# Hybrid trunk on one core: joined repairs, negated scores, one order of the attention on TensorE

## The chip, the cores and the metric

One core of a Trainium2 chip runs the kernel. Its engines are TensorE (PE in the profile; its weight loads are PEld), VectorE (DVE), ScalarE (ACT), GpSimd (POOL) and SyncE (SP), which issues the DMA transfers here. The metric is the device time of one launch in microseconds, as the median of several runs.

## The reference

The kernel computes two layers of a trunk over 256 latent tokens `x` and 256 context tokens `h`, with a width of 1024. In each layer every part is normalized and modulated, `_rms_norm(x, g) * (1 + scale) + shift`, where shift, scale and gate are nine vectors that come from `silu(c) @ ada_w[l] + ada_b[l]`:

```python
x = x + 0.5 * m[2] * swiglu(modulate(x, norm_g[l, 0], m[0], m[1]), w1, w3, w2)      # width 2816
o = concat(hgrn2(...), neighbourhood_attention(...), sliding_window_attention(...)) # of modulate(x) @ w_in
x = x + m[5] * (o @ w_out[l])
x = x + 0.5 * m[8] * swiglu(modulate(x, norm_g[l, 2], m[6], m[7]), ...)
```

The context goes the same way, and in the last layer only as far as the latents need it. Neighbourhood attention (NA) has six heads of 64: a latent query sees all four rows of its grid, within a row the columns of a window of 16, and all context keys; its scores are `q·k/8 + bias`, with a bias `na_rpb` by relative position and a mask of −1e30 elsewhere. Sliding-window attention (SW) has six query heads on two key heads, rotary positions, a window of 128 to each side and one sink score for each head that enters the softmax's maximum and sum. All inputs are float32.

## The kernel before, in words

The program is written out by hand, line by line, and a scheduler orders it when the kernel is built: it goes by the program's order, by dependences and by priorities. Pools (28 slots, 12 half tiles, four PSUM tiles `mm` for products, four `aux`) decide when a tile is free again. What the program pins (`keep_in_program_order`) keeps its place on its engine.

**Products.** Each float32 product is three matmuls on rounded parts (`mm3`, L222 to L226): whi·h, wlo·h and whi·(rest of h), 128x512 each over eight steps k. `Stream` (L68) reads weights in transfers of up to 1 MB into three buffers; `convert` (L100) makes a unit's `whi` on ScalarE (L109) and `wlo` on VectorE (L110), some five units ahead.

**Startup** (`body`, L1071; `boot`, L1153; `first`, L418). x and context are transposed on TensorE, eight groups of four into `xps` (L1140), and copied by VectorE into `xT` (L1142). Then VectorE's short chain gives `rs` (L397 to L402), which `rbc` spreads over partitions (L1274). `ada_direct` (L308) makes one block of 512 modulation columns: eight matmuls `adaps` with the transferred `adaraw` (L314), a ScalarE copy `adaev`, four small matmuls `adap` (L320) and VectorE's additions. Blocks 2 and 0 are scale and shift of the first four steps k, blocks 3 and 1 those of the last four. `first` multiplies four units at once: for k = 0 it calls `boot(0)`, for k = 4 `boot(1)`.

**FFN** (`ffn`, L475). Pairs of product groups for w1 and w3; ScalarE's silu (L522), VectorE's product `silu` (L523), the split `g` (L219, L220), then w2. Beside it runs `side`: `ada_gen` (L323) accumulates further modulation columns on VectorE (`adaacc`, L347 and L349) with matmuls at the end of each, and `load_bias(l)` (L1039) reads layer l's bias: one transfer into `scr`, 24 transfers `bias<-scr` on the SP queue (L1051), and one POOL instruction of 128x3072 that adds the column mask `colmask` (L1054). `tick` takes steps of these jobs by credits.

**Mixer** (`mixer`, L1015). `proj_hg` first; then `weave` mixes three threads by their costs: projections (`proj_v_na` L627, `proj_sw` L686, `w_out` L970), `hgrn` (L723), and `attention` (L873) for "na", then "sw", with an earlier priority. Attention goes over units (j, qt): head pairs j = 0 to 2, query tiles qt of 128, 0 and 1 latent, 2 and 3 context (mixer 1 has only the first two). `stage_s` makes a head's scores (two matmuls, `ks` and `kls`, L891 and L892) and the softmax: VectorE adds bias or mask and takes the maximum (L903, into a half tile `sb`; for context L908), makes it negative (L910; with the sink L913), ScalarE's exponential with the sum (L914), the reciprocal (L918) and the scale (L919). `stage_t` transposes P (`pt`, L927) and copies it to `ptsb`, on ScalarE for the first head of a pair (L930), on VectorE for the second (L932). `stage_v` multiplies by V into `ot` (L946), and the last unit of a pair is split into `o`. In a step, for each head the scores of unit i and the transposes of unit i − 1 follow each other, then stage_v of unit i − 2. Some lines of it:

```python
            for hh in range(2):
                if i < n:
                    stage_s(i, hh)
                    yield 0.5
                if 0 <= i - 1 < n:
                    stage_t(i - 1, hh)
                    yield 0.5
            if 0 <= i - 2 < n:
                stage_v(i - 2)
                yield 0.9
```

## Time and profile before

| | |
|---|---|
| time, median of 3 runs | 1890.07 us (1888.53 to 2241.34) |
| the profiled execution's own time | 1889.66 us |
| its span | 1887.9 us |
| TensorE busy | 1839.9 us, 97% |
| VectorE, ScalarE, POOL busy | 67%, 38%, 7% |
| chain that ended last | PE 89%, DVE 4%, ACT 2%, DMA 2% |

The profile is of one execution. A row of the timeline has the start in us from the span's start, its duration, the engine, the line of the kernel, the operation with its output and inputs, how often it is repeated and, in brackets, the engine's idle time before it and what ended that. Times of successive matmuls overlap in these rows, so the distance of starts tells their pace. The clock is the share of full speed that TensorE was granted.

### The profile page before, as it was taken

The page shows a single profiled execution, that of the slowest core. Times are in us where ns is not written, and L with a number is a line of the kernel's source. Part 1 is how long each engine was busy: PE and PEld are TensorE (multiplying, and loading weights), DVE is VectorE, ACT ScalarE, POOL GpSimd, SP SyncE. Part 2 cuts the span into 40 slices and gives each one's busy share as a digit, 9 for nine tenths or more (in the row PEclk, how much of TensorE's full clock was granted, in tenths as well). Part 3 has the DMA queues.
Part 4 walks back from the last instruction along what each step waited for, and adds up shares of the span by engine and source line. Part 5 has one row for each costly group of instructions (what it writes and reads, how often), then busy time and mean ns, then how long its engine had stood idle before and what let it go on. Part 6 is the DMA issues. An engine that isn't in the chain of part 4 may idle for free.

```text
span 1887.9 us, 27747 instructions
## 1 busy us (share of the span) xinstructions
PE 1839.9 (97%) x11071; PEld 1521.7 (81%) x11071; DVE 1266.0 (67%) x2341; ACT 725.2 (38%) x1214; POOL 138.5 (7%) x199
## 2 busy tenths in 40 slices
PE   7999999999999899999999999999999999999998
PEld 4777778789777679778777897777888977789998
DVE  4696668766777778867567675565333757887554
ACT  4322222235346457322222362222123635665443
POOL 0100000030400102000000110000001140020000
PEclk9999999999999999999999999999999999999999
DMA  9664545532211123645445426564222321146651
GB/s 346 197 218 148 184 156 178 168 116 69 74 49 40 34 71 102 214 154 192 142 146 193 128 86 205 171 203 161 90 95 76 120 68 38 43 154 203 214 168 56
DMA packets 233642, 258.24 MB, mean 137 GB/s; under 512 B 18886, under 2 KB 195370, under 8 KB 233258
## 3 DMA queue, kind: packets, MB, share of 16 engines
q1 hardware_dynamic: 233514, 256.48, 42.4%
q8 instruction: 87, 1.43, 0.3%
q14 instruction: 41, 0.34, 0.1%
HBM read 255.41 MB, written 2.48 MB: 137 GB/s over the span
## 4 chain that ended last, share of the span: by engine, by line
PE 89%; DVE 4%; ACT 2%; DMA 2%; issue 1%; SPq 1%; POOL 1%; DVEq 0%; ACTq 0%; POOLq 0%
PE mm L224 27%; PE mm L225 27%; PE mm L226 26%; PE ot L946 2%; PE pt L927 1%; DMA adaraw<-in_ada_w_dram 1%; PE adaps L359 1%; PE s L891 1%; DVE adaacc L349 1%; PE s L892 1%; PE lv L747 1%; POOL k L774 1%; ACT whi L109 1%; DVE P L919 0%; DMA raw<-in_ffn_w_dram 0%
## 5 line engine op out<-in xcount | busy, mean ns | idle before, releaser
L224 PE MATMUL mm<-h,whi 128*128 128x512 f32 (+1 forms) x1632 | 594.6, 365 | 5.4 <-DVE silu L523 3.2
L225 PE MATMUL mm<-h,wlo 128*128 128x512 f32 (+1 forms) x1632 | 590.4, 362 | 0.0
L226 PE MATMUL mm<-h,whi 128*128 128x512 f32 (+1 forms) x1632 | 589.4, 361 | 0.0
L110 DVE TENSOR_TENSOR wlo<-raw,whi 128x1024 fp32r<-128x1024 f32 (+2 forms) x344 | 400.2, 1184 | 90.5 <-ACT whi L109 75.5
L109 ACT ACTIVATE whi<-raw 128x1024 fp32r<-128x1024 f32 (+2 forms) x344 | 338.8, 1012 | 291.7 <-PE mm L225 131.1
L224 PEld LDWEIGHTS mm<-h,whi 128*128 128x128 f32 x1632 | 307.8, 189 | 68.1 <-issue 12.6
L225 PEld LDWEIGHTS mm<-h,wlo 128*128 128x128 f32 x1632 | 308.1, 189 | 50.3 <-issue 1.5
L226 PEld LDWEIGHTS mm<-h,whi 128*128 128x128 f32 x1632 | 308.0, 189 | 50.2 <-issue 0.2
L349 DVE SCALAR_TENSOR_TENSOR adaacc<-adaraw,s,adaacc 128x512 f32<-128x512 f32 x392 | 281.6, 763 | 40.4 <-DMA adaraw<-in_ada_w_dram 39.1
L224 PE MATMUL mm<-g,whi 128*128 128x512 f32 (+1 forms) x740 | 265.1, 358 | 0.0
L226 PE MATMUL mm<-g,whi 128*128 128x512 f32 (+1 forms) x740 | 263.7, 356 | 0.0
L225 PE MATMUL mm<-g,wlo 128*128 128x512 f32 (+1 forms) x740 | 263.5, 356 | 0.0
L219 ACT ACTIVATE g<-silu 128x512 fp32r<-128x512 f32 (+1 forms) x92 | 51.4, 562 | 317.4 <-DVE silu L523 284.5
L523 DVE TENSOR_TENSOR silu<-mm,silu 128x512 f32<-128x512 f32 (+1 forms) x80 | 50.0, 629 | 165.1 <-PE mm L226 139.0
L415 DVE SCALAR_TENSOR_TENSOR xT<-mm,mod,xT 128x256 f32<-128x256 f32 x216 | 96.7, 479 | 94.1 <-PE mm L226 93.3
L224 PEld LDWEIGHTS mm<-g,whi 128*128 128x128 f32 x740 | 139.1, 188 | 24.9 <-ACT whi L109 2.5
L225 PEld LDWEIGHTS mm<-g,wlo 128*128 128x128 f32 x740 | 139.1, 188 | 21.7
L226 PEld LDWEIGHTS mm<-g,whi 128*128 128x128 f32 x740 | 139.1, 188 | 21.6
L1243 POOL CAST hp<-mod 128x2 fp32r<-128x2 f32 x40 | 22.7, 598 | 1114.3 <-PE mm L225 339.0
L522 ACT ACTIVATE silu<-mm 128x512 f32<-128x512 f32 (+1 forms) x80 | 42.6, 547 | 132.0 <-PE mm L226 132.0
L220 DVE TENSOR_TENSOR g<-silu,g 128x512 fp32r<-128x512 f32 (+1 forms) x92 | 54.8, 603 | 32.1 <-ACT g L219 31.8
L1225 POOL TENSOR_TENSOR ssq<-ssq,sq 128x256 f32<-128x256 f32 x50 | 44.5, 904 | 302.9 <-ACT sq L1222 302.8
(210 smaller groups left out, 2008.3 us busy)
## 6 DMA issues: line engine op xcount, KB each, us to landing
raw<-in_ffn_w_dram SPq DMA_DIRECT2D x120, 1024.0 KB, 5.5
adaraw<-in_ada_w_dram SPq DMA_DIRECT2D x144, 512.0 KB, 5.0
raw<-in_ffn_w_dram SPq DMA_DIRECT2D x16, 768.0 KB, 5.0
raw<-in_w_in_dram SPq DMA_DIRECT2D x12, 1024.0 KB, 5.1
raw<-in_w_in_dram SPq DMA_DIRECT2D x16, 512.0 KB, 5.1
raw<-in_w_out_dram SPq DMA_DIRECT2D x8, 640.0 KB, 3.9
bias<-scr SPq DMA_DIRECT2D x48, 64.0 KB, 2.4
raw<-in_w_in_dram SPq DMA_DIRECT2D x4, 768.0 KB, 4.6
```

Of the source, the lines that this page charges most:

```text
L109: K.nc.scalar.activation(hi, v, AF.Copy)
L110: K.nc.vector.tensor_tensor(out=lo, in0=v, in1=hi.bitcast(F32), op=OP.subtract)
L219: self.nc.scalar.activation(hi, src, AF.Copy)
L220: self.nc.vector.tensor_tensor(out=lo, in0=src, in1=hi.bitcast(F32), op=OP.subtract)
L224: mmul(ps, whi, ahi, start=start, stop=False)
L225: mmul(ps, wlo, ahi, start=False, stop=False)
L226: mmul(ps, whi, alo, start=False, stop=stop)
L349: nc.vector.scalar_tensor_tensor(acc[:, t], w, sc, acc[:, t], op0=OP.mult, op1=OP.add)
L415: self.nc.vector.scalar_tensor_tensor(self.x[:, d, sl], ps[:, sl], self.mod[l][:, m, d, s:s + 1], self.x[:, d, sl], op0=OP.mult, op1=OP.add)
L522: nc.scalar.activation(a[:, 0:n], ps[i][:, 0:n], AF.Silu)
L523: nc.vector.tensor_tensor(out=a[:, 0:n], in0=ps[2 + i][:, 0:n], in1=a[:, 0:n], op=OP.mult)
L1225: eng.tensor_tensor(out=self.ssq[s], in0=self.ssq[s], in1=t, op=OP.add)
```

## The change

Four parts, and an order for each.

1. Startup. `pinned` makes matmuls, transposes and conversions keep program order. Only four groups of x transposes stand ahead of `rs`; two follow block 2, two block 0, the last two with late copies. `ada_direct` loses its second half to `ada_columns`, called later. k 0 to 3 of units 0 and 1 come first, and blocks 3 and 1 are laid among k 0 to 3 of units 2 and 3.
2. Bias. The POOL instruction goes; VectorE makes `bias = colmask − bias` in six pinned pieces of 128x512 in each layer. The `scr` transfer is pinned too. The side jobs are 2 to 4, bias, 5 to 8 instead of 2 and 3, bias, 4 to 8, and the bias costs more credits.
3. Signs. Scores, masks, bias and sink are stored negated (q is scaled by −0.125), so that VectorE takes a minimum and the exponential gets scale −1; the instruction that made the maximum negative goes for "na". P overwrites the masked scores in place of `sb`. `hgrn` uses `K2` for its output instead of a new slot.
4. Attention on TensorE. Scores wait (without a semaphore, `behind`) for the fourth k of the projection after theirs (`R.marks`), transposes for the last scores issued. A step makes both heads' scores, then both heads' transposes; `stage_v` takes two units at a time, heads 1, 0, pinned. Both copies to `ptsb` are ScalarE's.

```diff
-            for k in range(KC):
-                if k == 0:
-                    us = norm.boot(0)
-                elif k == 4:
-                    norm.boot(1)
-                    norm.bounds()
-                for u, p in zip(us, ps):
-                    self.mm3(p, u[0][:, k], u[1][:, k], norm.h[k][:, 0], norm.h[k][:, 1], k == 0, k == KC - 1)
+            for k in range(4):
+                prod(k, 0, 1)
+            scale = norm.block(3)
+            prod(0, 2, 3)
+            self.ada_columns(0, 3, scale)
+            prod(1, 2, 3)
+            prod(2, 2, 3)
+            shift = norm.block(1)
+            prod(3, 2)
+            self.ada_columns(0, 1, shift)
+            prod(3, 3)
+            norm.boot2()
+            norm.bounds()
+            for k in range(4, KC):
+                prod(k, 0, 1, 2, 3)
+                self.st.pump()
...
-                    R.q["na"] += self.stack_q(ps, n, 0.125)
+                    R.q["na"] += self.stack_q(ps, n, -0.125)
...
-            nc.tensor.matmul(ps[:, 0:nk], q[:, qs], k[:, k0:k0 + nk], start=True, stop=False)
-            nc.tensor.matmul(ps[:, 0:nk], q[:, qs], kl[:, k0:k0 + nk], start=False, stop=True)
+            ins = nc.tensor.matmul(ps[:, 0:nk], q[:, qs], k[:, k0:k0 + nk], start=True, stop=False)
+            if qt == 0 and hh == 0:
+                self.behind(ins, R.marks[mark(i)])
+            last.append(nc.tensor.matmul(ps[:, 0:nk], q[:, qs], kl[:, k0:k0 + nk], start=False, stop=True))
...
-                src = self.half("sb")
+                src = P
...
-                                               scalar=-3e38, op0=OP.add, op1=OP.max, accum_out=mx)
+                                               scalar=3e38, op0=OP.add, op1=OP.min, accum_out=nmx)
...
-            if kind == "na":
-                nc.vector.tensor_scalar(nmx, mx, -1.0, None, op0=OP.mult)
-            else:
+            if kind == "sw":
                 sk = self.sink[:, l * 6 + h:l * 6 + h + 1]
-                nc.vector.tensor_scalar(nmx, mx, sk, -1.0, op0=OP.max, op1=OP.mult)
-            nc.scalar.activation(P[:, 0:nk], src[:, 0:nk], AF.Exp, bias=nmx, accum_out=tot)
+                nc.vector.tensor_scalar(nmx, nmx, sk, None, op0=OP.min)
+            nc.scalar.activation(P[:, 0:nk], src[:, 0:nk], AF.Exp, bias=nmx, scale=-1.0, accum_out=tot)
...
-            if hh == 0:
-                nc.scalar.activation(pt[:, 0:nk], ps[:, 0:nk], AF.Copy)
-            else:
-                nc.vector.tensor_copy(pt[:, 0:nk], ps[:, 0:nk])
+            nc.scalar.activation(pt[:, 0:nk], ps[:, 0:nk], AF.Copy)
...
+            for hh in range(2):
                 if 0 <= i - 1 < n:
                     stage_t(i - 1, hh)
                     yield 0.5
-            if 0 <= i - 2 < n:
-                stage_v(i - 2)
-                yield 0.9
+            if i >= 3 and i % 2 == 1:
+                stage_v((i - 2, i - 3))
+                yield 1.8
...
-        nc.gpsimd.tensor_tensor(out=self.bias[:, 0:12, :], in0=self.bias[:, 0:12, :], op=OP.add,
-                                in1=self.colmask[:, None, :].to_broadcast([128, 12, 256]))
+        for h in range(6):
+            b = self.bias[:, 2 * h:2 * h + 2, :]
+            self.tc.keep_in_program_order(
+                nc.vector.tensor_tensor(out=b, in0=self.colmask[:, None, :].to_broadcast([128, 2, 256]), in1=b,
+                                        op=OP.subtract))
+            yield 1
...
-        self.ada_it = self.side((0, [2, 3]), (0, None), (0, [4, 5, 6, 7, 8]))
+        self.ada_it = self.side((0, [2, 3, 4]), (0, None), (0, [5, 6, 7, 8]))
```

TensorE at startup, from `rbc` to the first product matmuls, before (`adaps` are the eight matmuls of a block, in the order 2, 0, 3; `adap` its columns):

```order
L1274 MATMUL rbc<-cc,rs 128x128 x4
L314 MATMUL adaps<-adaraw,s_153 32x512 x8
L320 MATMUL adap_251<-cc,adaev 128x2 x4
L314 MATMUL adaps<-adaraw,s_153 32x512 x8
L320 MATMUL adap_269<-cc,adaev 128x2 x4
L314 MATMUL adaps<-adaraw,s_153 32x512 x8
L224 MATMUL mm<-h,whi 128x512 x2
```

And after the change (all matmuls of the helper stand at L227, `xps` at L1197):

```order
L1354 MATMUL rbc<-cc,rs 128x128 x4
L227 MATMUL adaps<-adaraw,s_153 32x512 x8
L1197 MATMUL xps<-cc,xraw 128x128 x8
L227 MATMUL adaps<-adaraw,s_153 32x512 x8
L227 MATMUL adap_247<-cc,adaev 128x2 x4
L227 MATMUL adap_258<-cc,adaev 128x2 x4
L1197 MATMUL xps<-cc,xraw 128x128 x8
L227 MATMUL mm<-h,whi 128x512
```

The third block, whose matmuls stood right ahead of the first product, has moved behind 24 of them, and half of the x transposes have moved in behind `rbc`.

TensorE in mixer 0, where the first attention units stand, before (`s_` are score tiles, one for each head and unit, `mm_4301` a projection, `pt_` transposes of P):

```order
L892 MATMUL s_4327<-kls_4292,qs_4200 128x512
L224 MATMUL mm_4301<-h_3186,whi_4104 128x512
L225 MATMUL mm_4301<-h_3186,wlo_4105 128x512
L226 MATMUL mm_4301<-h_3186,whi_4104 128x512
L892 MATMUL s_4316<-kls_4292,qs_4200 128x512
L224 MATMUL mm_4301<-h_3187,whi_4104 128x512
L225 MATMUL mm_4301<-h_3187,wlo_4105 128x512
L226 MATMUL mm_4301<-h_3187,whi_4104 128x512
L224 MATMUL mm_4301<-h_3188,whi_4104 128x512
L225 MATMUL mm_4301<-h_3188,wlo_4105 128x512
L226 MATMUL mm_4301<-h_3188,whi_4104 128x512
L927 MATMUL pt_4338<-cc_83,P_4309 128x128 x4
```

And after the change:

```order
L227 MATMUL mm_4283<-h_3170,whi_4086 128x512
L933 MATMUL s_4310<-ks_4273,qs_4182 128x512
L936 MATMUL s_4310<-kls_4274,qs_4182 128x512
L933 MATMUL s_4319<-ks_4273,qs_4182 128x512
L933 MATMUL s_4328<-ks_4273,qs_4182 128x512
L936 MATMUL s_4328<-kls_4274,qs_4182 128x512
L933 MATMUL s_4337<-ks_4273,qs_4182 128x512
L936 MATMUL s_4319<-kls_4274,qs_4182 128x512
L936 MATMUL s_4337<-kls_4274,qs_4182 128x512
L969 MATMUL pt_4346<-cc_83,P_4314 128x128 x4
L969 MATMUL pt_4353<-cc_83,P_4323 128x128 x4
L933 MATMUL s_4360<-ks_4273,qs_4182 128x256
```

The projection matmuls that stood between the scores and the first transposes have moved ahead of the scores; eight score matmuls of two units now stand in a row, and the transposes follow them.

VectorE in the second FFN after the change, where layer 1's mask goes on (`bias<-cc,bias`; `silu` and `g` belong to the FFN's products):

```order
L557 TENSOR_TENSOR silu<-mm,silu 128x512
L222 TENSOR_TENSOR g<-silu,g 128x512
L110 TENSOR_TENSOR wlo<-raw,whi 128x1024
L1110 TENSOR_TENSOR bias<-cc,bias 128x512
L110 TENSOR_TENSOR wlo<-raw,whi 128x1024
L1110 TENSOR_TENSOR bias<-cc,bias 128x512 x4
L110 TENSOR_TENSOR wlo<-raw,whi 128x1024
L1110 TENSOR_TENSOR bias<-cc,bias 128x512
L365 TENSOR_SCALAR adaacc<-adaraw,s_153 128x512 x2
```

Before, POOL did this in mixer 0, behind the last hgrn instructions of that mixer:

```order
L774 TENSOR_TENSOR k_3144<-k_3144,tot 128x16x16 x2
L774 TENSOR_TENSOR k_3145<-k_3145,tot 128x16x16 x2
L774 TENSOR_TENSOR k_3144<-k_3144,tot 128x8x32 x2
L774 TENSOR_TENSOR k_3145<-k_3145,tot 128x8x32 x2
L1054 TENSOR_TENSOR bias<-bias,cc 128x3072
L1243 CAST hp<-mod_141 128x2 x2
```

It has moved from POOL to VectorE and from mixer 0 to the FFN behind it.

## Rows read from the trace of the kernel before

**Rows 1.** The head of the page and its first part.
```profile
span 1887.9 us, 27747 instructions
...
PE 1839.9 (97%) x11071; PEld 1521.7 (81%) x11071; DVE 1266.0 (67%) x2341; ACT 725.2 (38%) x1214; POOL 138.5 (7%) x199
```

**Rows 2.** Waits of TensorE by releaser: total us, times, longest us.
```profile
PE pt L927 <- DVE sm L918: 7.4, 2, 5.4
PE lv L747 <- DVE q L774: 3.7, 3, 2.0
```

**Rows 3.** Timeline, startup: start us, us, engine line op out<-in xcount [idle before <-releaser].
```profile
13.47 2.48 DVE L1142 COPY xT<-xps 128x512 f32<-128x512 f32 x4
...
28.60 1.05 PE L314 MATMUL adaps<-adaraw,s 128*32 128x512 f32 x4 [1.73 <-DMA adaraw<-in_ada_w_dram]
...
30.16 4.62 DVE L110 TENSOR_TENSOR wlo<-raw,whi 128x1024 fp32r<-128x1024 f32 x4
...
33.55 0.74 PE L224 MATMUL mm<-h,whi 128*128 128x512 f32 x2
```

**Rows 4.** Timeline, around k = 4 of the first group.
```profile
49.57 1.05 PE L320 MATMUL adap<-cc,adaev 128*128 128x2 f32 x8 [0.77 <-ACT adaev L317]
...
52.22 0.79 PE L224 MATMUL mm<-h,whi 128*128 128x512 f32 x1 [1.60 <-ACT h L1293]
```

**Rows 5.** Timeline, SP's queue, VectorE and TensorE in the first FFN.
```profile
51.17 14.81 SPq L1051 DMA_DIRECT2D bias<-scr  x17
...
80.78 9.96 DVE L349 SCALAR_TENSOR_TENSOR adaacc<-adaraw,s,adaacc 128x512 f32<-128x512 f32 x5
...
102.98 0.77 PE L224 MATMUL mm<-h,whi 128*128 128x512 f32 x1 [3.23 <-DVE silu L523]
```

**Rows 6.** Timeline, end of mixer 0's attention: repair, scale, transpose.
```profile
631.46 6.99 POOL L1054 TENSOR_TENSOR bias<-bias,cc 128x3072 f32<-128x3072 f32 x1 [122.21 <-DMA bias<-scr]
...
631.95 6.65 DVE L919 TENSOR_SCALAR P<-P,sm 128x256 f32<-128x256 f32 x1
...
638.75 0.66 PE L927 MATMUL pt<-cc,P 128*128 128x128 f32 x2 [5.36 <-DVE sm L918]
```

**Rows 7.** Timeline, one head's softmax chain in mixer 0.
```profile
536.41 0.42 PE L892 MATMUL s<-kls,qs 128*128 128x512 f32 x1
...
536.86 0.69 DVE L903 CUSTOM_DVE_ANT_1 sb<-s,bias 128x512 f32<-128x512 f32 x1 [0.59 <-PE s L892]
...
538.55 1.28 ACT L914 ACT_TABLE_LOAD   x1 [1.05 <-DVE sm L910]
...
539.84 0.72 ACT L914 ACTIVATE P<-sb,sm 128x512 f32<-128x512 f32 x1
...
542.31 0.63 PE L927 MATMUL pt<-cc,P 128*128 128x128 f32 x4 [1.16 <-DVE P L919]
```

**Rows 8.** Windows: A:B length, busy us (x count) by engine, PEclk, DMA share, GB/s.
```profile
105.00:110.00 5.00, 5.00 (x16) 3.94 (x15) 5.00 (x7) 2.88 (x4) 0.00 (x0) 0.61 0.33 120
...
640.00:645.00 5.00, 5.00 (x22) 3.00 (x22) 1.77 (x8) 1.29 (x5) 0.00 (x0) 0.52 0.01 3
```

**Rows 9.** Timeline of TensorE, last neighbourhood attention units in mixer 0.
```profile
623.77 0.70 PE L717 MATMUL rot<-swraw,cc 128*128 128x256 f32 x2 [0.69 <-ACT swraw L701]
...
627.97 0.43 PE L946 MATMUL ot<-ptsb,v 128*64 128x128 f32 x2 [1.46 <-ACT ptsb L930]
628.33 0.51 PE L224 MATMUL mm<-o,whi 128*128 128x512 f32 x1
628.68 0.40 PE L225 MATMUL mm<-o,wlo 128*128 128x512 f32 x1
628.91 0.39 PE L226 MATMUL mm<-o,whi 128*128 128x512 f32 x1
```

**Rows 10.** Lines: copies of transposed tiles; xcount | busy us, mean ns | idle before.
```profile
L932 DVE COPY ptsb<-pt 128x512 f32<-128x512 f32 (+1 forms) x36 | 21.4, 595 | 11.2 <-PE pt L927 11.2
...
L930 ACT ACTIVATE ptsb<-pt 128x512 f32<-128x512 f32 (+1 forms) x36 | 18.5, 515 | 10.4 <-PE pt L927 10.1
```

178 lines of the change are left out of this document (117 added, 61 removed).

## Prediction

> **What bounds the kernel now.** I read the page first: TensorE is busy for 1839.9 of the span's 1887.9 us [rows 1]. So the time is TensorE's own work, the 48 us in which it waits, and the work that it does at the lower granted clock after a wait. The change leaves the number of TensorE instructions as it is (10051 in the order before and after), so it can win only the 48 us, the clock, and the small price of going from one kind of matmul to another. Next I read the waits of TensorE, summed by who ended them: the largest are transposes of P behind a VectorE instruction and hgrn's `lv` behind VectorE and, through it, POOL [rows 2]. Then I went through the timeline at each pause: the startup [rows 3, 4], one pause in the first FFN [rows 5] and the end of mixer 0's attention [rows 6]. Last the windows, for the clock: 105 to 110 us ran at a mean of 0.61 and 640 to 645 us at 0.52, with TensorE busy all the time [rows 8]. The level in between is a mixture of 1.2 and 2.4 GHz; a busy window of 5 us at mean c has lost (1 − c) × 5 us, so 1.95 and 2.4 us here. Each of these two windows follows a pause of TensorE of over 3 us.
>
> The profiled execution took 1889.66 us, 0.4 less than the median of the runs shown; the sum below starts from it.
>
> **Startup.** Before, the x transposes' eight copies stand ahead of the chain that gives `rs`, which the scale of every h needs; the last four take 2.48 us from 13.47 [rows 3]. With four of them moved behind, `rs` comes some 2.4 us earlier, and with it the columns and h; by nothing if the adaraw transfers are what is late. No wait on them stands in the rows before 28.60, so I take the earlier h. The first product matmul stands at 33.55 because all eight matmuls of block 3 stand ahead of it in program order and wait for adaraw from 28.60 on [rows 3]. Afterwards 24 product matmuls (k 0 to 3 of two units) stand ahead of block 3. They need h, and whi and wlo of two units; wlo x4 ran from 30.16 for 4.62 us [rows 3], so I let them begin at 29. Up to k = 4 TensorE then has 48 product matmuls of 0.23 us (11.1 us; spacing in [rows 9]), blocks 3 and 1 of twice 1.05 us [rows 3] (4.2), two sets of columns of 1.05 [rows 4] (2.1), with 3 to 6 matmuls laid over each adaev copy, and I add 1.2 for the clock, half of what the worse window lost [rows 8]: 18.6 us. So k = 4 starts at about 47.6, where it was 52.22 after pauses of 0.77 and 1.60 us [rows 4]: −4.6. After 52.22 the clock was lower for a while too; of a loss like that of [rows 8] I count 1.4, since a pause remains. **Startup −6** (bounds: −1, if transfers and conversions set the start, and −8).
>
> **The repairs.** Before, POOL adds the column mask in one instruction of 128x3072, once for each layer. The second one runs 6.99 us from 631.46, and a VectorE scale of 128x256 that starts at 631.95 takes 6.65 us, nearly as long as POOL's own instruction; TensorE then waits 5.36 us for the reciprocal behind it [rows 6]. The price of this place is 5.36 us, and of clock half of the 1.25 us to 640 and then 2.4 [rows 8]: 8.4 us. The Trainium skill ("SBUF — State Buffer", section "Who interferes with whom") says that the port pair that VectorE shares with GpSimd is locked for a whole instruction; by that rule the 6.65 us are a blocked VectorE, and the trace agrees. The first repair falls into the first FFN: five adaacc instructions that start at 80.78 take 9.96 us, 2 us each, of which by POOL's row above some 6 us are the lock; VectorE has no gap from there on, and the silu product of the next tile frees its PSUM buffer so late that TensorE waits 3.23 us until 102.98 [rows 5]. Clock: from 102.98 to 105 half of 2.0 us, and 1.95 in the next window [rows 8], together 2.9. Without the lock VectorE is 6 us earlier, and the adaraw transfers no longer stand behind 17 bias transfers that kept the SP queue from 51.17 for 14.81 us [rows 5]; together that is more than the 3.23 us and the 5 by which TensorE itself is now earlier. **FFN −6.1** (bounds 0 and −6.1).
>
> In their place stand twelve VectorE subtractions of 128x512. The nearest row is the attention's add of the same shape, one operand of it in PSUM, 0.69 us [rows 7]: 6 × 0.7 = 4.2 us for each layer. They stand in FFN(0,0) and FFN(0,1), among wlo conversions, where VectorE has room (67% busy over the span [rows 1]) and the silu product has a second pair of PSUM buffers, 48 matmuls or 11 us. I take 0; without that cover 3.2 us (the pause of [rows 5] again) plus its clock. The bias transfers are now pinned behind ada's and in the second FFN instead of mixer 0: nothing in the mixer waited for them but POOL.
>
> **Scores, masks, copies.** Negation drops 36 one-column instructions from VectorE, one in each neighbourhood softmax chain, and the 36 `ptsb` copies of 595 ns go from VectorE, 21.4 us in all, to ScalarE, where the other 36 take 18.5 [rows 10]. Neither is the bound while projections lie between, so 0 by itself; it counts where nothing lies between.
>
> **The order on TensorE.** Counted over the two orders, changes into a projection matmul from another kind of work fall from 147 to 117, into scores of 512 columns from 52 to 29, into transposes from 71 to 56. A matmul after such a change is followed by the next after 0.35 us instead of 0.23 [rows 9]: 30 × 0.12 = 3.6 us, and for the rest 0 to 1.5. **−4** (bounds 0 and −5).
>
> The price is that the attention's work now stands together. In mixer 0 (call it cluster A) eight score matmuls stand in a row, then eight transposes, with no projection between. Read the chain of one head before: second score matmul 536.41, reduction 536.86 (0.69), table load 538.55 (1.28), exponential 539.84, transposes at 542.31 [rows 7]. That is 5.9 us, in which TensorE did 13 projection matmuls beside scores, and waited only 1.16. Afterwards it has six score matmuls there (1.4 us). The one-column instruction falls out and the scale follows at once, so I put the chain at 5.4 us: 4.0 of waiting to the first transposes. After them each further head costs ScalarE 0.72 for the exponential [rows 7], now the copy's 0.52 in the mean [rows 10], and the readout of its sum, some 1.4 us, against 0.6 of transposes: three more waits, 2.2 us with the scores between. So 6.2 against 1.16: +5.0, and +2.0 of clock (a little under the 2.4 of the window after 638.75). A second such place (B) stands at the end of neighbourhood attention in mixer 0, with `rot` ahead of it; by the same count 6.7 us of waiting, where before 0.69 at 623.77 and 1.46 at 627.97 [rows 9] remain when POOL's is taken out: +4.5, and +1.5 of clock. Mixer 1 has only the latent half; its largest waits are on `lv` [rows 2], which the change does not touch: +0.5. **Mixers: −8.4 + 7.0 + 6.0 + 0.5 = +5.1** (bounds: −8.4, if the lists of ready work cover the chains after all, and +13).
>
> The Trainium skill ("ScalarE: Activation LUTs", section "What ACT_TABLE_LOAD costs") puts a table switch at about 1283 ns for the load and 1380 for a drain, 2.66 us together. Here the exponential starts 0.01 us after the load's 1.28 [rows 7], so the drain does not lie behind it; by the page's figure the first P of cluster A would come 1.4 us later and the sum would be −9.6. The trace decides, and the sum goes without it.
>
> **Sum:** −6 − 6.1 − 4 + 5.1 = −11.0; 1889.66 − 11.0 = 1878.7, and with the 0.4 to the median 1879.
>
> **The rivals.**
> (1) *The clusters hide.* For it: TensorE's queue after a cluster could hold w_out or the next projection, and halves, now without `sb`, allow more heads in flight. Against it: the order is fixed at build time, and there are no projection matmuls in either cluster. Then the mixers give −8.4: −6 − 6.1 − 4 − 8.4 = −24.5, so 1865.
> (2) *Startup is set by transfers.* For it: adaraw transfers are waited for from 28.60 on [rows 3], and each transfer lands when it did. Against it: the 24 matmuls ahead of block 3 do not need them. Then the startup gives −1: 1884.
> (3) *Slower: every group of attention units pays its whole chain.* One mechanism, the uncovered softmax chain, at four places (A, B and the two groups of mixer 1): 5.4 of waiting and 3.0 of clock each, 33.6 us, less the 3.3 waited before: −6 − 6.1 − 4 − 8.4 + 30.3 = +5.8, so 1896. It decides once three of the four are fully open (25.2 − 3.3 against 24.5 of gains: about even). For it: 1.4 us of ScalarE for each head against 0.6 of TensorE. Against it: mixer 1 has hgrn and w_out work to lay between.
> (4) *The negation and copies do nothing, and the order gives nothing back* (the change does not do what it says in the mixers, while POOL's lock goes): −6 − 6.1 − 8.4 = −20.5, 1870; it lies between the forecast and (1).
>
> **How the numbers follow.** Chances: the forecast 0.48 (its own range 1873 to 1884: the clusters' clock ±3, the switches ±2), (1) 0.14, (4) 0.13, (2) 0.13, (3) 0.10, and 0.02 for anything else. The range leaves out half of (1), half of (3) and the rest: 1864 to 1892. A change of 2% is 37.8 us, about what a measurement of this kernel can tell from no change. No case reaches −37.8 (that would need nearly all 48 us of waiting) or +37.8: faster 0.03, same 0.96, slower 0.01.
>
> **What would show it.** Startup: the first matmul of k = 4 at about 47, and product matmuls ahead of block 3's. FFN: no pause near 95 to 100, no VectorE instruction of 128x256 or 128x512 longer than 1.5 us anywhere, no clock below 1 there. Clusters: two stretches in mixer 0 with 6 to 7 us of waits of transposes on P and of `ot` on `ptsb`, and a window below 0.8 after each. Wrong would be: k = 4 no earlier than 51 (startup), a new pause on `silu` or `wlo` in either FFN (repairs), or under 3 us of waiting in the clusters, which is (1).

## The result, and the profile after

The changed kernel takes 1864.49 us (median of 4 runs, 1864.01 to 1864.73) against 1889.30 before: a ratio of 0.9873, with an interval of 0.9857 to 0.9888. One of the four runs before took 2241.34 us, and the ratio leaves it out. The gain is 24.8 us, where 11 were forecast; the time lies at the very edge of the range. The profiled span fell from 1887.9 to 1862.2 us.

The page of the changed kernel, its head, the busy times and the chain:

```profile
span 1862.2 us, 27738 instructions
...
PE 1818.4 (98%) x11071; PEld 1512.3 (81%) x11071; DVE 1237.2 (66%) x2281; ACT 739.9 (40%) x1250; POOL 125.5 (7%) x198
...
PE 90%; DVE 5%; ACT 2%; issue 1%; POOL 1%; DMA 1%; SPq 0%; DVEq 0%; ACTq 0%; POOLq 0%
```

TensorE is busy for 21.5 us less (1839.9 in [rows 1]) with the same 11071 instructions, and it waits for only some 4 us less. So most of the gain is not waiting that went, but the same matmuls in less time: a better clock and less lost from one matmul to the next. The traces give the share of each as an estimate: TensorE was busy at the lower granted clock (1.2 GHz) for 31.1 us before and for 16.5 after, half of which is lost, so 7.3 us are clock; the remaining 14 us are the pace of the matmuls. The waits of TensorE (total us, times, longest us):

```profile
PE adap L384 <- ACT adaev L380: 3.9, 5, 0.8
PE lv L786 <- DVE q L813: 3.7, 3, 2.0
PE s L936 <- DVE kls L720: 3.6, 4, 1.4
...
PE mm L227 <- DVE wlo L110: 2.4, 4, 1.0
PE s L933 <- ACT ks L718: 2.2, 3, 1.0
...
PE pt L969 <- DVE sm L960: 1.8, 2, 1.5
```

The wait of transposes on VectorE fell from 7.4 to 1.8 us, `lv` kept its 3.7 [rows 2], and new ones came: `adap` behind its own ScalarE copy, and scores behind `kls` and `ks`.

To see where the time went, both traces are cut at the same product matmuls (their order among themselves is that of the program, 8496 in all). Each number is the time from one cut to the next, in us:

| from, to | before | after | difference | forecast |
|---|---|---|---|---|
| start to product 150 (startup) | 78.66 | 73.20 | −5.5 | −6 |
| to 300 (the first pause in the first FFN) | 42.67 | 36.42 | −6.3 | −6.1 |
| to 1950 (rest of the first FFN, begin of mixer 0) | 359.37 | 356.67 | −2.7 | 0 |
| to 2850 (mixer 0) | 288.64 | 277.52 | −11.1 | about +2 |
| to 6000 (the two FFNs between) | 711.75 | 716.33 | +4.6 | 0 |
| to 7050 (mixer 1) | 223.73 | 219.24 | −4.5 | about −1 |
| to the last product | 173.36 | 173.10 | −0.3 | 0 |

The first two lines came as worked out; the mixers did not. The third line is work that moved: the matmuls of one ada module, some 2.2 us, stand in mixer 0 after the change (e5 moves them back); a wait of 0.8 for its `adap` is gone. In the forecast's column the prediction's −4 for the order is shared out between the mixers by their units. In the startup the first product stands at 26.37 and k = 4 at 49.08, where 33.55 and 52.22 were [rows 3, 4]:

```profile
14.39 2.07 PE L1354 MATMUL rbc<-cc,rs 128*128 128x128 f32 x8 [2.86 <-DVE rs L420]
...
26.37 0.79 PE L227 MATMUL mm<-h,whi 128*128 128x512 f32 x1 [0.91 <-ACT h L1373]
...
49.08 0.50 PE L227 MATMUL mm<-h,whi 128*128 128x512 f32 x1 [0.78 <-ACT h L1373]
```

And there is no pause left in the first FFN; windows of the changed kernel (busy us and instruction counts of PE, PEld, DVE, ACT, POOL, then the clock):

```profile
85.00:95.00 10.00, 10.00 (x45) 8.10 (x44) 9.51 (x13) 4.81 (x6) 0.00 (x0) 1.00 0.63 211
95.00:105.00 10.00, 10.00 (x48) 7.20 (x47) 6.92 (x12) 2.58 (x5) 0.00 (x0) 1.00 0.55 183
```

TensorE is busy throughout at a clock of 1.00, where before it waited 3.23 us and then ran a window at 0.61 [rows 5, 8].

The place that the prediction called cluster A, on ScalarE and TensorE:

```profile
525.38 0.59 ACT L717 ACTIVATE ks<-mm 64x512 fp32r<-64x512 f32 x1 [4.00 <-PE mm L227]
...
526.62 0.49 PE L933 MATMUL s<-ks,qs 128*128 128x512 f32 x1 [1.05 <-ACT ks L718]
...
528.04 0.79 PE L936 MATMUL s<-kls,qs 128*128 128x512 f32 x1 [0.92 <-DVE kls L720]
...
529.27 1.22 PE L933 MATMUL s<-ks,qs 128*128 128x512 f32 x2 [0.44 <-ACT ks L718]
...
533.81 1.09 PE L969 MATMUL pt<-cc,P 128*128 128x128 f32 x4 [1.53 <-DVE sm L960]
```

Three waits for `ks` and `kls` (1.05, 0.92, 0.44) stand ahead of the wait for P (1.53): 4.2 us with one of 0.24 further on, where 6.2 were forecast and 1.16 were before [rows 7]. The first row is the odd one: ScalarE waits 4.00 us for a matmul before it makes `ks`, though the product that `ks` copies was finished 24 matmuls earlier (before, and in e4 and e5 below, `ks` starts one matmul behind its product). Cluster B, for which 6.7 us were forecast:

```profile
610.99 0.70 PE L756 MATMUL rot<-swraw,cc 128*128 128x256 f32 x2 [0.69 <-ACT swraw L740]
...
612.45 1.04 PE L969 MATMUL pt<-cc,P 128*128 128x128 f32 x8
...
614.97 1.23 PE L969 MATMUL pt<-cc,P 128*128 128x128 f32 x8 [0.92 <-ACT ptsb L973]
```

That is 1.6 us, less than the 0.69 and 1.46 of [rows 9]: the eight transposes at 612.45 start 0.2 us behind the last scores of the new unit, so they are those of a unit before, and they cover the new unit's chain.

The wait that nobody expected, in the second FFN:

```profile
767.58 1.06 PE L377 MATMUL adaps<-adaacc,ones 128*32 128x512 f32 x8
768.82 0.60 ACT L380 ACTIVATE adaev<-adaps 128x512 f32<-128x512 f32 x1 [15.60 <-PE adaps L377]
...
769.47 0.66 PE L384 MATMUL adap<-cc,adaev 128*128 128x128 f32 x4 [0.83 <-ACT adaev L380]
```

`adaps` and `adap` of a module stand directly behind each other, so TensorE waits 0.83 us for the copy between them. Of the sixteen modules that go through VectorE five are like this, where one was before; elsewhere 24 product matmuls stand between the two.

### The profile page after: what moved, and what is told of

It reads as the page before. It is cut to its first block, busy times and chain, and to the rows that moved or that the text cites. A ratio compares the mean times of both kernels' runs of the same rounds, so it can differ in the third digit from the quotient of the medians.

```text
span 1862.2 us, 27738 instructions
## 1 busy us (share of the span) xinstructions
PE 1818.4 (98%) x11071; PEld 1512.3 (81%) x11071; DVE 1237.2 (66%) x2281; ACT 739.9 (40%) x1250; POOL 125.5 (7%) x198
## 3 DMA queue, kind: packets, MB, share of 16 engines
q8 instruction: 87, 1.43, 0.3%
## 4 chain that ended last, share of the span: by engine, by line
PE 90%; DVE 5%; ACT 2%; issue 1%; POOL 1%; DMA 1%; SPq 0%; DVEq 0%; ACTq 0%; POOLq 0%
PE mm L227 82%; PE ot L990 1%; PE pt L969 1%; PE adaps L377 1%; DVE wlo L110 1%; PE s L933 1%; PE s L936 1%; POOL k L813 1%; DVE kls L720 0%; PE adaps L227 0%; PE lv L786 0%; ACT whi L109 0%; PE adap L384 0%; DVE P L947 0%; DMA xraw<-in_ctx_dram 0%
## 5 line engine op out<-in xcount | busy, mean ns | idle before, releaser
L227 PE MATMUL mm<-h,whi 128*128 128x512 f32 (+1 forms) x3264 | 906.7, 362 | 3.3 <-ACT h L1373 1.7
L227 PEld LDWEIGHTS mm<-h,whi 128*128 128x128 f32 x3264 | 580.4, 188 | 112.1 <-issue 5.7
L227 PE MATMUL mm<-h,wlo 128*128 128x512 f32 (+1 forms) x1632 | 588.0, 360 | 0.5 <-DVE wlo L110 0.5
L227 PE MATMUL mm<-g,whi 128*128 128x512 f32 (+1 forms) x1480 | 402.6, 357 | 0.0
L227 PEld LDWEIGHTS mm<-h,wlo 128*128 128x128 f32 x1632 | 307.0, 188 | 50.0 <-DVE wlo L110 1.0
L367 DVE SCALAR_TENSOR_TENSOR adaacc<-adaraw,s,adaacc 128x512 f32<-128x512 f32 x392 | 275.3, 748 | 39.2 <-DMA adaraw<-in_ada_w_dram 38.2
L227 PEld LDWEIGHTS mm<-g,whi 128*128 128x128 f32 x1480 | 261.7, 188 | 47.4 <-ACT whi L109 4.2
L227 PE MATMUL mm<-g,wlo 128*128 128x512 f32 (+1 forms) x740 | 263.5, 356 | 0.0
L227 PEld LDWEIGHTS mm<-g,wlo 128*128 128x128 f32 x740 | 139.2, 188 | 21.8
L227 PE MATMUL mm<-hp,whi 128*128 128x258 f32 x384 | 73.0, 286 | 0.5 <-ACT whi L109 0.3
L227 PE MATMUL mm<-o,whi 128*128 128x256 f32 (+1 forms) x280 | 67.6, 327 | 0.0
L227 PE MATMUL mm<-whi,h 128*128 128x256 f32 (+1 forms) x256 | 64.9, 346 | 0.4 <-ACT k L640 0.4
L227 PEld LDWEIGHTS mm<-hp,whi 128*128 128x128 f32 x384 | 60.5, 190 | 1.1 <-ACT whi L109 0.7
```

Source lines behind the costliest of these rows:

```text
L227: ins = self.nc.tensor.matmul(*args, **kw)
L367: nc.vector.scalar_tensor_tensor(acc[:, t], w, sc, acc[:, t], op0=OP.mult, op1=OP.add)
```

## The experiments

The first four undo one part each in the changed kernel.

**e1: the attention's order of before.**

```diff
-            return i >= len(units) or len(R.marks) > mark(i)
+            return i >= len(units) or len(R.q[kind]) > 2 * units[i][0] and len(R.k[kind]) > 2 * units[i][0]
...
-            if qt == 0 and hh == 0:
-                self.behind(ins, R.marks[mark(i)])
-                if c == 0:
-                    self.behind(ins, last[-1])
-                    for hh in (1, 0):
+                    for hh in range(2):
-                        if not first:
-                            self.tc.keep_in_program_order(ins)
...
-            for hh in range(2):
                 if 0 <= i - 1 < n:
                     stage_t(i - 1, hh)
...
-            if i >= 3 and i % 2 == 1:
-                stage_v((i - 2, i - 3))
+            if 0 <= i - 2 < n:
+                stage_v((i - 2,))
```

> The changed kernel with the attention's order of before: scores and transposes head by head, stage_v for one unit at a time, heads 0, 1, no marks. Everything else stays changed. Theory P (the price of changing between kinds of matmul was put too low: a trip from a projection into ot and back costs about 0.35 us, of which the prediction counted 0.12): ot runs rise from 21 to 46 on TensorE, 25 x 0.35 = 8.7, scores and transposes 2 to 3 more, less some 4 us of waits and clock of cluster A: 5 to 9 us slower than the changed kernel, 1870 to 1873. Theory L (the gain in the mixers is the work taken from VectorE: 36 copies, 36 one-column instructions, POOL's lock; the order is worth about 0 to 3 us less clusters, as the prediction had it): -4 to +2, 1860 to 1866.

Measured: 1871.92 us, ratio 0.9914 (0.9899 to 0.9929); about 7.7 us slower than the changed kernel, as theory P said. Cut as above, mixer 0 takes 284.06 (+6.5), mixer 1 219.26 (0.0). The waits in mixer 0 are almost the same in both (9.17 and 9.15 us). What grew is the time from one matmul to the next: summed over the 288 `ot` matmuls of mixer 0 it is 23.76 us, against 18.19 with the new order. With waits and clock taken out, e1's mixer 0 is 8.4 us longer: 5.8 in `ot`, 2.1 in scores, 1.6 in products, 0.5 in the rest, less 1.6 in transposes. Mixer 1's 0.0 is a sum too: 2.5 us of slower pace and 2.6 us less waiting. Rows of e1's TensorE show a run of two:

```profile
593.68 0.38 PE L967 MATMUL pt<-cc,P 128*128 128x128 f32 x2
594.08 0.43 PE L986 MATMUL ot<-ptsb,v 128*64 128x128 f32 x2
594.44 0.50 PE L227 MATMUL mm<-h,whi 128*128 128x512 f32 x1
594.77 0.39 PE L227 MATMUL mm<-h,wlo 128*128 128x512 f32 x1
```

The two `ot` take 0.36 us until the next matmul starts, and that one 0.33 instead of 0.23. In the changed kernel 28 stand in a row:

```profile
540.28 1.75 PE L990 MATMUL ot<-ptsb,v 128*64 128x128 f32 x28
541.96 0.77 PE L830 MATMUL kTps<-cc,k 128*128 128x128 f32 x5
```

They take 1.68 us, 0.06 each: two heads' matmuls of a pair run beside each other. Counted over mixer 0's starts, `ot` has 35 runs in e1 and 14 in the changed kernel. The last of a run is followed after 0.20 us in the median of both, where within runs the mean is 0.066 in e1 and 0.055 in the changed kernel; a projection matmul is followed by `ot` after 0.327 in the median, by its like after 0.233; and 144 pairs instead of 116 start within 0.03 us of each other. Some half of the growth in `ot` is the 21 exits more, the other half are pairs that no longer start together; no run separates the grouping from the pinned alternation of the heads.

**e2: stage_v for one unit.**

```diff
-            if i >= 3 and i % 2 == 1:
-                stage_v((i - 2, i - 3))
-                yield 1.8
+            if 0 <= i - 2 < n:
+                stage_v((i - 2,))
+                yield 0.9
```

> The changed kernel with stage_v for one unit instead of two. Theory P: ot runs rise from 21 to 30, 9 x 0.35 = 3.2 us, 1867.5 (1866.5 to 1868.5). Theory L: 9 x 0.12 = 1.1, or less where TensorE waits anyway, 1864.5 to 1865.6.

Measured: 1861.23 us, ratio 0.9859 (0.9844 to 0.9874), faster than the changed kernel, though the intervals overlap. Both theories missed. Mixer 0 has 23 runs of `ot` instead of 14, and their sum rose by only 0.96 us, 0.11 a run: the new runs stand mostly between transposes and scores, not between projections. So 0.35 is not the price of any run, but of a trip from a projection and back. The gain is in mixer 1, 215.18 against 219.24: the waits for `kls` and `ks` at the head of its attention (1.43, 0.74 and 0.99 in the changed kernel) are gone, and TensorE runs at the full clock there, where 3.1 us of its work were at the lower one.

**e3: the startup of before** (`first`, `boot`, `ada_direct` and the x transposes as in [rows 3]'s kernel).

```diff
-            for k in range(4):
-                prod(k, 0, 1)
-            scale = norm.block(3)
-            prod(0, 2, 3)
...
+            for k in range(KC):
+                if k == 0:
+                    us = norm.boot(0)
+                elif k == 4:
+                    norm.boot(1)
```

> The changed kernel with the startup of before (eight x transposes ahead of rs, block 3 ahead of the first products). As the prediction had it: +5.6 to +6, and the second product group of k = 4 back at 52. Two more of the pairs of ada matmuls stand next to each other, up to +1.6. 1870 to 1872. If the gain at the start is lost again in the first FFN because its transfers set the pace: +0 to +2.

Measured: 1871.32 us, ratio 0.9909 (0.9892 to 0.9926), 6.8 us slower. Its first product waits behind block 3 again, and k = 4 behind the last:

```profile
28.25 5.01 PE L329 MATMUL adaps<-adaraw,s 128*32 128x512 f32 x16 [1.24 <-DMA adaraw<-in_ada_w_dram]
...
49.20 1.05 PE L335 MATMUL adap<-cc,adaev 128*128 128x2 f32 x8 [0.77 <-ACT adaev L332]
51.85 0.58 PE L227 MATMUL mm<-h,whi 128*128 128x512 f32 x1 [1.60 <-ACT h L1332]
```

By the cuts the startup itself is +4.2 us. Another 3.0 stand in mixer 1 (222.23), where TensorE's order is that of the changed kernel, kind by kind; more on that below.

**e4: the repairs on POOL**, with the transfers and ada jobs as before (the bias is `colmask − bias` there too).

```diff
-        for h in range(6):
-            b = self.bias[:, 2 * h:2 * h + 2, :]
-            self.tc.keep_in_program_order(
-                nc.vector.tensor_tensor(out=b, in0=self.colmask[:, None, :].to_broadcast([128, 2, 256]), in1=b,
-                                        op=OP.subtract))
-            yield 1
+        nc.gpsimd.tensor_tensor(out=self.bias[:, 0:12, :], in0=self.colmask[:, None, :].to_broadcast([128, 12, 256]),
+                                in1=self.bias[:, 0:12, :], op=OP.subtract)
...
-        self.ada_it = self.side((0, [2, 3, 4]), (0, None), (0, [5, 6, 7, 8]))
+        self.ada_it = self.side((0, [2, 3]), (0, None), (0, [4, 5, 6, 7, 8]))
```

> The changed kernel with POOL's one instruction for each layer's bias, the bias transfers unpinned and the ada jobs in the order of before. As the prediction had it: +6.1 in the first FFN, +8.4 at the place in mixer 0 if POOL's second instruction falls into the attention again. Four fewer pairs of ada matmuls stand next to each other, -3.2. So 1873 to 1876 with both places, 1867 with the first alone; about 1861 if neither lock delays TensorE.

Measured: 1868.88 us, ratio 0.9898 (0.9884 to 0.9913), 4.7 us slower. The first FFN's pause is back (42.77 to product 300, +6.35, as forecast), and so is the lock in mixer 0:

```profile
622.22 6.68 POOL L1105 TENSOR_TENSOR bias<-cc,bias 128x3072 f32<-128x3072 f32 x1 [117.16 <-DMA bias<-scr]
...
622.73 6.32 DVE L961 TENSOR_SCALAR P<-P,sm 128x256 f32<-128x256 f32 x1
...
629.18 1.12 PE L969 MATMUL pt<-cc,P 128*128 128x128 f32 x4 [4.76 <-DVE sm L960]
```

And yet mixer 0 is 2.0 us shorter than in the changed kernel (275.53), and the two FFNs between are back at 711.58. So the change's repair brought something along that costs: the five `adap` waits, and in mixer 0 something worth more than the lock. In e4 the first transposes of cluster A wait 0.48 us and none of the three waits for `ks` and `kls` stands there, under the new order of the attention. That spoke against the prediction's reason for cluster A, and gave theory S of e5. In the changed kernel one ada module is half done when mixer 0 begins: its two sums `adaacc` are made in the first FFN, and the matmuls that read them come only near mixer 0's end. They hold two of the 28 slots all that time, and `ks` and `kls` need slots. In e4, as in the kernel before, a module is half done too, but with only the first of its two sums begun (25% of its VectorE instructions), so one slot is held.

**e5: one number.**

```diff
-ADA_RATE = {(0, 0): 4.4, (0, 1): 4.0, (1, 0): 3.2, (1, 1): 3.2}
+ADA_RATE = {(0, 0): 4.8, (0, 1): 4.0, (1, 0): 3.2, (1, 1): 3.2}
```

> The changed kernel with one number changed: the side job's rate in the first FFN is 4.8 credits instead of 4.4. The ada module that was left half done at the mixer's start (its two sums keep two of the 28 slots all through mixer 0) is then done before. Theory S (cluster A's waits come from these slots: the copies ks and kls of the first pair wait for a slot): cluster A's waits fall from 4.2 us to under 1.5 and its clock loss of 3 to 3.5 us goes, and two of the five pairs of ada matmuls without work between them go (-1.6): 6 to 9 us faster than the changed kernel, ratio to before 0.9825 to 0.984. Theory C (the cluster waits because the softmax chain has nothing to cover it, whatever the slots): only the 1.6 us, ratio 0.9862 to 0.9868.

Measured: 1860.17 us, ratio 0.9856 (0.9842 to 0.9871), 3.2 us faster by the ratios, whose intervals overlap; between the two theories as a total, but not where they differ. Mixer 0 takes 269.79, 7.7 us less, of which some 2.2 are the module's own matmuls that moved to the FFN. Of cluster A's waits this is left:

```profile
532.86 1.22 PE L969 MATMUL pt<-cc,P 128*128 128x128 f32 x8 [0.49 <-DVE sm L960]
```

The clock over that place is 1.00 again, where it was 0.66 over 15 us (windows of e5, then of the changed kernel):

```profile
525.00:540.00 15.00, 14.40 (x98) 10.73 (x97) 10.69 (x32) 11.09 (x27) 0.00 (x0) 1.00 0.00 1
```

```profile
525.00:540.00 15.00, 10.79 (x42) 7.26 (x41) 9.84 (x30) 10.66 (x25) 0.00 (x0) 0.66 0.00 0
```

The next module is half done now, with its first sum made and its second not begun. So theory S holds here: two sums held go with the waits, one sum does not, and 10.79 us of work at a mean of 0.66 cost some 3.7 us more. That it is the slots is read from this; no trace shows which slot a tile gets. The rest of the gain was lost in mixer 1 (222.26, +3.0) at the same order and the same waits. e4 and e5 also have the same order in mixer 0, kind by kind, and differ there only in POOL's instruction: 275.53 − 269.79 = 5.7 us is what the lock costs.

**e6: the second head's copies on VectorE again.**

```diff
-            nc.scalar.activation(pt[:, 0:nk], ps[:, 0:nk], AF.Copy)
+            if hh == 0:
+                nc.scalar.activation(pt[:, 0:nk], ps[:, 0:nk], AF.Copy)
+            else:
+                nc.vector.tensor_copy(pt[:, 0:nk], ps[:, 0:nk])
```

> The changed kernel with the second head's ptsb copies on VectorE again (36 copies, 21.4 us). Theory L (VectorE's relief is what shortened mixer 1 by 4.5 us and a part of mixer 0): 3 to 6 us slower than the changed kernel, ratio 0.989 to 0.9905. Theory P (the order's fewer changes of kind are what shortened it, VectorE is not the bound): within 1 us of the changed kernel, ratio 0.9868 to 0.9878, or faster, since ScalarE is what the clusters wait for.

Measured: 1875.87 us, ratio 0.9938 (0.9921 to 0.9955), 11 to 12 us slower, more than either theory gave. Mixer 0 is +2.6, mixer 1 +8.8. In mixer 1 two transposes wait for VectorE's scale, where the changed kernel has 0.37 at most:

```profile
1637.44 1.71 PE L969 MATMUL pt<-cc,P 128*128 128x128 f32 x8 [1.92 <-DVE P L961]
...
1646.76 1.31 PE L969 MATMUL pt<-cc,P 128*128 128x128 f32 x8 [1.91 <-DVE P L961]
```

So under the new order VectorE's copies do stand in the way; the windows of 5 us around these waits ran at 0.82 to 0.84. Of mixer 1's 8.8 us, some 3 are waiting and some 5 are clock.

**e7: e5 and e2 together**, rate 4.8 and stage_v for one unit.

```diff
-            if i >= 3 and i % 2 == 1:
-                stage_v((i - 2, i - 3))
+            if 0 <= i - 2 < n:
+                stage_v((i - 2,))
...
-ADA_RATE = {(0, 0): 4.4, (0, 1): 4.0, (1, 0): 3.2, (1, 1): 3.2}
+ADA_RATE = {(0, 0): 4.8, (0, 1): 4.0, (1, 0): 3.2, (1, 1): 3.2}
```

> Rate 4.8 and stage_v for one unit: the two edits that gave or should give something, together. If they add: the gain of the rate (6 to 9 by theory S, 1.6 by theory C) and 3 us of the single stage_v, whose gain stood in mixer 1: ratio 0.981 to 0.9825 (S), 0.985 (C). If both remove the same wait, no more than the better of them.

Measured: 1856.39 us, ratio 0.9835 (0.9821 to 0.9850). The edits add, if to a little less than theory S put: mixer 0 270.30, mixer 1 218.05. This one is faster than both kernels of the case.

**e8: a one-column instruction more in each neighbourhood chain** (a multiplication by 1 between the minimum and the exponential).

```diff
+            if kind == "na":
+                nc.vector.tensor_scalar(nmx, mx, 1.0, None, op0=OP.mult)
```

> The changed kernel with a one-column VectorE instruction put back into each of the 36 neighbourhood softmax chains (it multiplies the minimum by 1). As the prediction had it: 0, but where the chain lies open (cluster A's first P, and waits of pt on sm) each adds 0.15 to 0.2 us: 0 to +1 us on the changed kernel, ratio 0.9872 to 0.988. If the negation is a part of mixer 1's 4.5 us: +2 to +4, ratio over 0.9885.

Measured: 1869.40 us, ratio 0.9905 (0.9890 to 0.9920), some 5 to 6 us slower. By the expectation this would speak for the negation, but the cuts don't: mixer 0 is +0.5, mixer 1 +3.3, and in mixer 1 the waits are those of the changed kernel to within 0.1 us each. What differs there is the clock, some 2.8 of the 3.3 us. I don't take this run as a price of the instruction.

The last four: three parts alone in the kernel before, and one more try.

**e9: the order alone.** The new order holds more heads at once. So e9 also has the room of the change: P in place of `sb`, and `K2` for hgrn's output. No run has the order without that room.

```diff
-                src = self.half("sb")
+                src = P
...
-        two = self.slot([128, 2, 512], F32, "hgout")
-        ob, og = two[:, 0], two[:, 1]
+        ob, og = K2[:, 0], K2[:, 1]
```

> The kernel before with the attention's order of the change and the room that it needs (P in place of sb, K2 in place of hgout), nothing else: startup, POOL's repair, signs and copies as before. Theory P (the order's price of a change was put too low): 6 to 7 us in mixer 0 and 2 to 3 in mixer 1 less than before, ratio 0.995 to 0.9962. As the prediction had it (the order costs more waits than it saves: +12 - 4 = +8 us): ratio 1.004. If the order helps only together with ScalarE's copies, since VectorE's copies hold it back: ratio 0.997 to 1.002.

Measured: 1882.64 us, ratio 0.9971 (0.9959 to 0.9982). Mixer 0 takes 282.15, −6.5 as in e1 from the other side, though POOL's lock holds the new order up longer than the old one (5.36 us in [rows 6]):

```profile
634.56 0.66 PE L950 MATMUL pt<-cc,P 128*128 128x128 f32 x2 [6.13 <-DVE sm L941]
```

Mixer 1 gains nothing as a sum (223.88): its pace is 4.1 us better and its waits are 4.8 us longer, those for `kls` and `ks` at the head of its attention and the waits of transposes on P again that e6 showed.

**e10: the copies alone.**

```diff
-            if hh == 0:
-                nc.scalar.activation(pt[:, 0:nk], ps[:, 0:nk], AF.Copy)
-            else:
-                nc.vector.tensor_copy(pt[:, 0:nk], ps[:, 0:nk])
+            nc.scalar.activation(pt[:, 0:nk], ps[:, 0:nk], AF.Copy)
```

> The kernel before with all ptsb copies on ScalarE. If VectorE's relief counts by itself, as undoing it in the changed kernel cost 10 us: 3 to 10 us faster, ratio 0.9947 to 0.998. As the prediction had it: 0, ratio 0.9985 to 1.0015.

Measured: 1888.51 us, ratio 1.0003 (0.9993 to 1.0012). As forecast, 0: with projections between the heads TensorE hardly waits for VectorE's copies. Its worth in e6 exists only under the new order.

**e11: repairs, pinned transfer and ada jobs alone.**

```diff
-        nc.gpsimd.tensor_tensor(out=self.bias[:, 0:12, :], in0=self.bias[:, 0:12, :], op=OP.add,
-                                in1=self.colmask[:, None, :].to_broadcast([128, 12, 256]))
+        for h in range(6):
+            b = self.bias[:, 2 * h:2 * h + 2, :]
+            self.tc.keep_in_program_order(
+                nc.vector.tensor_tensor(out=b, in0=self.colmask[:, None, :].to_broadcast([128, 2, 256]), in1=b,
+                                        op=OP.add))
+            yield 1
...
-        self.ada_it = self.side((0, [2, 3]), (0, None), (0, [4, 5, 6, 7, 8]))
+        self.ada_it = self.side((0, [2, 3, 4]), (0, None), (0, [5, 6, 7, 8]))
```

> The kernel before with the repairs on VectorE, the pinned bias transfer and the new order of the ada jobs. As the prediction had it: -6.1 in the first FFN and -8.4 in mixer 0, 14.5 us together. By what undoing it showed: -6.3 in the first FFN, -7.8 for the lock in mixer 0, +4 for ada pairs with nothing between them, and the slots that the half done ada module keeps through mixer 0: +3 to +6. So -4 to -7, ratio 0.9963 to 0.998; by the prediction alone 0.9925.

Measured: 1885.63 us, ratio 0.9989 (0.9979 to 0.9998); less than even the smaller expectation. The first FFN has its −6.2, POOL's place is gone, and cluster A's waits are there under the old order of the attention:

```profile
530.47 0.50 PE L891 MATMUL s<-ks,qs 128*128 128x512 f32 x1 [1.05 <-ACT ks L681]
531.89 0.50 PE L892 MATMUL s<-kls,qs 128*128 128x512 f32 x1 [0.92 <-DVE kls L683]
533.12 0.73 PE L891 MATMUL s<-ks,qs 128*128 128x512 f32 x2 [0.73 <-ACT ks L681]
...
534.81 0.78 PE L892 MATMUL s<-kls,qs 128*128 128x512 f32 x1 [0.73 <-DVE kls L683]
538.16 1.08 PE L927 MATMUL pt<-cc,P 128*128 128x128 f32 x4 [2.56 <-DVE P L919]
```

Mixer 0 ends at 288.11, only 0.5 less than before, and the two FFNs between are +4.6. So these waits in mixer 0 belong to the ada jobs' new order, not to the attention's.

**e12: rate 5.0 and one unit** (with e2's edit).

```diff
-ADA_RATE = {(0, 0): 4.4, (0, 1): 4.0, (1, 0): 3.2, (1, 1): 3.2}
+ADA_RATE = {(0, 0): 5.0, (0, 1): 4.0, (1, 0): 3.2, (1, 1): 3.2}
```

> The changed kernel with rate 5.0 and stage_v for one unit. Rate 4.8 left three of five pairs of ada matmuls without work between them; 5.0 leaves one: 1.6 us less than the run with 4.8 and one unit, ratio 0.9825 to 0.983; the lower clock after a wait in mixer 1 may come or go with it, 3 us either way.

Measured: 1860.43 us, ratio 0.9855 (0.9838 to 0.9871), a miss. The FFNs between are the shortest of all (710.78), as expected, but mixer 0 takes 277.95, and the waits for `kls` and `ks` are back:

```profile
384.68 0.74 DVE L367 SCALAR_TENSOR_TENSOR adaacc<-adaraw,s,adaacc 128x512 f32<-128x512 f32 x1
```

```profile
532.23 0.51 PE L936 MATMUL s<-kls,qs 128*128 128x512 f32 x1 [1.31 <-DVE kls L720]
533.46 0.73 PE L933 MATMUL s<-ks,qs 128*128 128x512 f32 x2 [0.73 <-ACT ks L718]
```

```profile
732.11 2.74 DVE L367 SCALAR_TENSOR_TENSOR adaacc<-adaraw,s,adaacc 128x512 f32<-128x512 f32 x4 [0.83 <-DMA adaraw<-in_ada_w_dram]
```

Rate 5.0 brings the next module so far that its second sum, too, is begun before mixer 0 (the last `adaacc` at 384.68) and ended only behind its attention (732.11), so two sums are held again. All fourteen traces divide by this count: two sums are held through mixer 0 in the changed kernel, e1, e2, e3, e6, e8, e11 and e12, and in each of them the first units wait for `ks` and `kls`; one is held in the kernel before, e4, e5, e7, e9 and e10, and none of them does.

## Why the prediction missed, by its own steps

**Startup: right in mechanism, some 2 us too large.** −6 forecast, −5.5 measured, −4.2 by e3 alone. The −5.5 sets the shortest trace against the longest: the nine traces with the new startup take 73.2 to 74.6 us to product 150, the five with the old one 77.4 to 78.7, so −3.8 in the mean. The first product came earlier than put (26.37, not 29) and at a lower clock, and k = 4 at 49.08 instead of 47.6; the window after it no longer loses clock. The range's lower end (transfers set the start) did not come about.

**Repairs: right in both places, with a cost not seen.** The first FFN gave 6.3 of 6.1. The lock in mixer 0 is 5.7 us by e4 against e5, where 8.4 were put; the wait was 4.76 us instead of the 5.36 of [rows 6], and the clock after it cost less. In the first FFN the lock is not spread over five instructions of 2 us, as the prediction read it: one `adaacc` took 7.31 us. The twelve VectorE subtractions take 0.684 us each (0.7 was put) and TensorE does not wait for them. But the same part of the change reordered the ada jobs, which the prediction read only as a question of transfers: five modules whose two matmul groups stand together (+3.9 us in the FFNs between), and two slots held through mixer 0 instead of one.

**The order on TensorE: the step that failed.** Its price was read off the one row behind a change, 0.12 us, times 30 entries: −4, with an end of −5. The rows for the rest were in the trace. In [rows 9] the `ot` at 627.97 is followed after 0.36, two matmuls of which a pair takes 0.11 in a run: leaving `ot` costs some 0.25, twice what the entry was counted at. What the order is worth shows when each mixer's time is split. The table is an estimate from the traces, in us: waits are TensorE's idle time, clock is half of its busy time at the lower granted clock, and pace is the rest, the time from one matmul to the next.

| | mixer 0: waits, clock, pace | mixer 1: waits, clock, pace |
|---|---|---|
| before | 12.9, 4.8, 271.0 | 7.3, 3.4, 213.0 |
| changed | 9.2, 4.1, 264.3 | 9.9, 1.6, 207.8 |
| e1 (changed, old order) | 9.2, 2.2, 272.7 | 7.3, 1.7, 210.3 |
| e9 (before, new order) | 16.2, 2.6, 263.3 | 12.0, 2.9, 209.0 |

In pace the order is worth 8.4 and 2.5 us by e1, 7.7 and 4.1 by e9: 11 to 12 us in both mixers, where 4 were put. The 2.2 us of the moved module stand in mixer 0 of both the changed kernel and e1, and in neither of the other two. The new order also has a price that the prediction did not see: with `stage_v` for two units, scores in mixer 1 wait for `kls` and `ks` (1.43, 0.74 and 0.99 us in the changed kernel), and these waits are gone in e1 and with one unit (e2, e7, e12).

**The clusters: wrong in reason and size.** +13.0 were put for waits and clock of A and B. B does not wait, since transposes of the units before cover the chain; the prediction took the rows of one group as if nothing else were in flight. A does wait, 4.2 us and some 3.7 of clock, but not for an uncovered chain: with one sum held instead of two (e5) only 0.49 us of it is left, e11 brings it up under the old order, and e12 brings it back. The chain's length, read rightly off [rows 7], was not what counted.

**Copies: 0 alone (e10), not 0 together. Signs: not priced.** Under the new order the copies on VectorE cost 2.6 us in mixer 0 and waits of 3 us more, and clock, in mixer 1 (e6). The prediction said "it counts where nothing lies between" and then did not count it. The negation has no run that prices it, since e8's difference is mostly clock. The three parts alone give −5.5, +0.6 and −2.1 us by their ratios (e9, e10, e11), −7 together, and the startup 5; the change gives 24 to 25. The parts need each other: the order frees TensorE from changes, and with the copies on VectorE it loses part of that again in waits (e6, e9).

So rival (1) gave the time, 1865, and was given 0.14. Its sum was −24.5 with −8.4 for the lock and no clusters; what happened in its place is −5.7 for the lock, some −17 in the mixers for order, copies and clock together, and +9 for the slots (5.5 in mixer 0, the 7.7 of e5 less the module's own 2.2) and the ada pairs (3.9). The number is right there by accident. The measured time stands at the edge of the forecast's range, too, only because errors stand against each other: the order's gain was put too small and the clusters' cost too large, and the slots and pairs were not put at all; without their 9 us it would be some 1855 (an estimate; e7, which is rid of most of them and has `stage_v` for one unit, took 1856.39).

**What stays open:** mixer 1's −4.5 is −5.2 of pace, −1.9 of clock and +2.6 of waits. Of the pace, e1 gives back 2.5 and e9 alone brings 4.1; how the rest is shared between order, copies and signs no run shows. Why the clock comes out otherwise at the same order and the same waits is open too.

## What to carry to other kernels

When an engine is 97% busy, its gain is in the distance from one instruction to the next: take the starts of successive instructions by kind and next kind, and price a change of order by both sides of each change, not by the instruction behind it. Split a stage into waits, clock and pace before calling it unmoved: mixer 1 of e1 was two differences that cancelled. A wait for a copy at the head of a stage may be a wait for its buffer: look which tile holds the slot, and for how long, before the chain is blamed. And where a side job's order or rate changes, count what it leaves half done at the next stage's border, and the buffers that this holds.
